# Layer A's triangular inverse: forward substitution on 16x16 blocks with a merge to 32x32, in place of forward substitution on 32x32 blocks

## The chip, the core and the metric

The kernel runs on one core of one Trainium2 chip. A core has five engines, each with its own instruction queue: TensorE (PE; its weight loads are shown apart as PEld), VectorE (DVE), ScalarE (ACT), GpSimd (POOL) and SyncE (SP), which here issues every DMA. Each takes its instructions in the order in which the program put them and waits for another engine only through semaphores. The metric is the device time of one launch in microseconds. Three runs of the kernel before gave 2158.89, 2161.75 and 2168.25 us; the median, 2161.75 us, is what a change is held against.

## What is computed

Two layers over 1024 tokens of width 1024: layer A mixes tokens with a gated delta rule, layer B with a forgetting attention. Of layer A this matters here:

```
L = where(strict, einsum('bhncd,bhnsd->bhncs', kb, k) * decay, 0.0)
T = triangular_solve(eye + L, eye, left_side=True, lower=True, unit_diagonal=True)
u = T @ vb
w = T @ (kb * exp(g)[..., None])
...
v_new = u_n - einsum('bhcd,bhde->bhce', w_n, state)
o = einsum(q_n, state) + einsum(a_n, v_new)
state = state * gl_n + einsum(k_n, v_new)
```

So every chunk of every head needs the inverse of a unit lower triangular matrix before its state update can run, and the updates of one head run one after the other. The kernel uses chunks of 128 tokens (the reference's 64 is a choice of blocking with the same result) and so inverts 128x128 matrices.

## The kernel before

Layer A is cut into 16 units: two halves of the sequence (h, 512 tokens, four chunks each) times eight pairs of value heads (g). A unit holds eight 128x128 triangular matrices (two heads times four chunks), numbered u.

For each unit the kernel (1) projects k, q and two heads of v and convolves them (`proj_conv`, and `proj_tile` for the gate z): six tiles of 24 matmuls of 128x512, which accumulate in PSUM tile `mm`; (2) builds the matrices in `lm` (`prepk`, L835); (3) inverts their diagonal blocks (`invert_blocks`); (4) merges the blocks into the whole inverse `r` (`invert_merge`, tile `rmat`); (5) runs the chain over four chunks (`chain`: PSUM tiles `ch` and `co`, with `xp`, `vn`, `ve` and `state` between them); (6) normalises and stores (`finish`). Layer A's output projection follows, then layer B.

`invert_blocks` moves the 32 diagonal 32x32 blocks of a unit (eight matrices, four blocks each) through DRAM, so that one block lies in one partition (L996 writes `lb`, L999 loads `lr`). Four groups of 32 partitions hold copies, and each copy solves every fourth column of the inverse. Forward substitution is 31 steps of two DVE instructions: a product `xtmp` (L1009) and a subtraction from `xi` (L1013). Step j has up to j // 4 + 1 columns and 31 - j rows, so 8 to 76 elements per partition. The result goes through DRAM again (L1018 writes `rb`, L1025 loads it into the diagonal blocks of `rmat`).

`invert_merge` transposes three of the four blocks on DVE (L1035, into `tmat`), merges pairs of 32 into 64 in two batches of small matmuls with ACT copies behind each (`pp`, L1043 and L1044; `rmat`, L1057 and L1059; a DVE scaling at L1058), and 64 into 128 in two more (`pq`, L1070; `rmat`, L1078). All these matmuls go to PSUM tile `su`, which has two banks; transposes on PE go to tile `tr`, also two banks.

PE's order is written by a planner inside the kernel (`Flow`). It runs the stages above as generators with priorities, adds up an estimated PE cost in `flow.t`, and fills PE with projection matmuls, which have the lowest priority, while a stage waits. A `yield` of some nanoseconds is how long the planner thinks the other engines take before the stage may go on; `flow.bank` and `flow.free` say when a PSUM bank may be used again. A merge isn't planned earlier than `LAT` ns after its inversion was issued (`t["end"]`), and later stages wait for counters (`done["merge"] >= i - 1` for `prepk`). The other engines' order comes from the tile framework's scheduler. Nearly all matmuls carry the line of the helper that records them, L121 (L125 for transposes), so they are told apart by tile.

Of the kernel before, what the change touches and what calls it, by code (L numbers as in the profile page):

```python
# [8 lines left out]
F32 = mybir.dt.float32  # L9
F32R = mybir.dt.float32r  # L10
BF16 = mybir.dt.bfloat16
AF = mybir.ActivationFunctionType
ALU = mybir.AluOpType
AX = mybir.AxisListType

P = 128
D = 1024
# [21 lines left out]
Y_PV = 6500  # L39
Y_PM = 1850  # L40
Y_P2 = 13300
Y_M0 = 900
Y_M1 = 1050
Y_M2 = 1100
# [18 lines left out]
Y_TC = 1500  # L63
ZL = 3
HI = 3000
LAT = 50000
Y_PB = 2500
Y_WO = 250
Y_WH = 3450
# [18 lines left out]
R_M = 800  # L88
# [5 lines left out]
XP = 0  # L94


class Flow:
# [36 lines left out]
    def bank(self, key, bufs, alloc):  # L134
        ring = self.rings.setdefault(key, [0, [0.0] * bufs])
        while ring[1][ring[0] % bufs] > self.t:
            yield 150
        i = ring[0] % bufs
        ring[0] += 1
        ring[1][i] = 1e15  # L140
        ps = alloc()
        self.held.append((ps, ring[1], i))
        return ps

    def free(self, ps, delay):
        n = next(n for n, v in enumerate(self.held) if v[0] is ps)
# [25 lines left out]
def tile_trunk(  # L172
# [287 lines left out]
    with ExitStack() as sa:  # L460
# [3 lines left out]
        def at(shape, name, bufs=1, dt=F32):  # L464
            return pa.tile(shape, dt, name=name, tag=name, bufs=bufs)
# [7 lines left out]
        nw_h = at([P, 1], "nw_h")  # L473
        dt_b = at([P, 16], "dt_b")
        neg_a = at([P, 16], "neg_a")
        xid = at([P, 8, 32], "xid", 1, BF16)
        nc.gpsimd.memset(xid, 0.0)
        for q in range(4):
            nc.gpsimd.affine_select(
                out=xid[32 * q : 32 * q + 32], in_=xid[32 * q : 32 * q + 32],  # L480
                compare_op=ALU.not_equal, fill=1.0, base=-q,
                pattern=[[-4, 8], [1, 32]], channel_multiplier=0,
            )
        rmat = [at([P, 8, P], f"rmat{i}") for i in range(2)]
        tmat = [at([P, 8, 64], f"tmat{i}") for i in range(2)]
        for i in range(2):
            nc.gpsimd.memset(rmat[i], 0.0)
            nc.gpsimd.memset(tmat[i], 0.0)
        halo = at([P, 32, 3], "halo")
        state = [at([P, 2 * P], f"state{g}") for g in range(NG)]  # L490
        ht_h = xt_([P, KT, HALF], "ht_h", dt=F32R)
# [2 lines left out]
        def start_norm():  # L494
# [16 lines left out]
            banks = []  # L511
            for _ in range(2):
                banks.append((yield from acc_bank()))
            for n, b in ((0, "lr"), (1, "vt")):
                br = at([1, D], b, 1)
                nc.sync.dma_start(br, ada_b[0:1, n * D : n * D + D])
                acc = at([P, D], "d2", 2)
                for k in range(KT):
# [198 lines left out]
        def proj_all():  # L717
            for i in range(2 * NG):
                h, g = divmod(i, NG)
                if g == 0:  # L720
                    if h == 0:
                        yield from start_norm()
                        done["start"] = 1
                    else:
                        yield from hold(lambda: done["norm"] == 1)
                        load_norm()
                    gt = {}
                    flow.add(gates(h, gt), 1)
# [259 lines left out]
        def invert_blocks(t):  # L988
            lm = t["lm"]
            t["r"] = r = rmat[t["g"] % 2]  # L990
            U = 2 * CPH
            lb = dram.tile([U, 4, 32, 32], F32, name="lb", tag="lb", bufs=2)
            t0 = flow.t
            for b in range(4):
                sl = slice(32 * b, 32 * b + 32)
                nc.sync.dma_start(lb[:, b].rearrange("u i j -> i u j"), lm[sl, :, sl])  # L996
            lr = at([P, 32, 32], "lr", 1)
            for q in range(4):
                nc.sync.dma_start(  # L999
                    lr[32 * q : 32 * q + 32], lb.rearrange("u b i j -> (u b) i j")  # L1000
                )
            xi = at([P, 8, 32], "xi", 1)
            nc.gpsimd.tensor_copy(xi, xid)
            for j in range(31):
                m = j // 4 + 1
                n = 31 - j
                tmp = at([P, 256], "xtmp", 1)
                tv = tmp[:, 0 : m * n].rearrange("p (m n) -> p m n", n=n)
                (nc.gpsimd if XP else nc.vector).tensor_tensor(  # L1009
                    tv, bc(lr[:, j + 1 :, j], 1, m), xi[:, 0:m, j : j + 1].broadcast_to([P, m, n]),  # L1010
                    op=ALU.mult,
                )
                (nc.gpsimd if XP else nc.vector).tensor_tensor(  # L1013
                    xi[:, 0:m, j + 1 :], xi[:, 0:m, j + 1 :], tv, op=ALU.subtract
                )
            rb = dram.tile([U, 4, 8, 4, 32], F32, name="rb", tag="rb", bufs=2)
            for q in range(4):
                nc.sync.dma_start(  # L1018
                    rb[:, :, :, q, :].rearrange("u b m i -> (u b) m i"), xi[32 * q : 32 * q + 32]
                )  # L1020
            rbv = rb.rearrange("u b m q i -> u b (m q) i")
            yield from hold(lambda: done["core"] >= done["inv"] - 1)
            for b in range(4):
                sl = slice(32 * b, 32 * b + 32)
                nc.sync.dma_start(r[sl, :, sl], rbv[:, b].rearrange("u c i -> c u i"))  # L1025
            done["inv"] += 1
            t["end"] = max(flow.t + Y_R2, t0 + LAT)

        def invert_merge(t):
            lm, r, tm = t["lm"], t["r"], tmat[t["g"] % 2]  # L1030
            U = 2 * CPH
            for b in (0, 1, 2):
                sl = slice(32 * b, 32 * b + 32)
                c0 = 32 * (b % 2)
                nc.vector.transpose(tm[sl, :, c0 : c0 + 32], r[sl, :, sl])  # L1035
            pa_ = yield from pst("su", 2)
            pb_ = yield from pst("su", 2)
            pp = at([P, U, 32], "pp", 1)
# [689 lines left out]
```

## Time and profile before

| | us |
|---|---|
| runs of the kernel, median of three | 2161.75 (2158.89 to 2168.25) |
| the profiled execution, its own time | 2165.32 |
| span of its instructions, first to last | 2163.6 |
| mean granted TensorE clock | 0.938 of full speed |
| layer A's units (first merge at 202.7, last at 1165.2) | about 100 to 1180 |
| layer A's output projection and the start of layer B | about 1180 to 1440 |
| layer B and the last projection | 1440 to 2163.6 |

The profile is one execution; its own time is 3.57 us over the median of the runs, and 1.7 us of it lie outside the span. A page of the profile gives busy time by engine, the span in 40 slices, the chain of work that ended last (followed back from the last instruction to whatever released each step), and groups of instructions with their busy time, the mean duration of one, and the idle time of the engine ahead of them. Further views give the same for a window of time, the instructions in order of time, and the waits added up. Where the names of two tiles stand as `out<-in`, the first is written and the others are read.

### The profile page before, as it was taken

The numbers are of one execution on the slowest core, as the hardware profiler recorded it, in microseconds if no ns is written. First come the engines' busy times: TensorE is split into PE (matmuls) and PEld (weight loads), VectorE is DVE, ScalarE is ACT, GpSimd is POOL, SyncE is SP. The second block draws the span as 40 slices with busy tenths as digits, with TensorE's granted clock in tenths as the row PEclk, the third lists the DMA queues.
The fourth block names the chain that finished last, engine by engine and source line by source line (L and its number), as shares of the span: only waits on it lengthen the run. The fifth ranks groups of instructions, "written<-read, shape, count | busy, mean of one in ns | idle before, by whom it ended". The sixth has DMA issues, their size and how long they took to land.

```text
span 2163.6 us, 32167 instructions
## 1 busy us (share of the span) xinstructions
PE 1865.2 (86%) x10860; PEld 1543.0 (71%) x10860; DVE 1586.1 (73%) x3625; ACT 1047.5 (48%) x2530; POOL 800.8 (37%) x648
## 2 busy tenths in 40 slices
PE   4667788888878888888888878899999999999898
PEld 3545666666667666767777756688888898888676
DVE  7788888787876888788987676745665666566664
ACT  4244444445536354445554444425655556555631
POOL 4244334344444433344442465642312322322212
PEclk7878889999999989899999999999999999999999
DMA  6544333344333323233326667611101201111522
GB/s 247 164 139 122 88 107 103 86 120 121 105 98 114 108 69 86 73 99 89 103 76 205 223 203 262 204 55 61 64 25 53 66 25 54 59 35 48 173 76 93
DMA packets 168088, 232.86 MB, mean 108 GB/s; under 512 B 66858, under 2 KB 107074, under 8 KB 167924
## 3 DMA queue, kind: packets, MB, share of 16 engines
q1 hardware_dynamic: 167924, 230.82, 34.5%
q8 instruction: 85, 1.39, 0.3%
q14 instruction: 79, 0.65, 0.1%
HBM read 203.88 MB, written 26.88 MB: 107 GB/s over the span
## 4 chain that ended last, share of the span: by engine, by line
PE 43%; DVE 30%; DMA 10%; issue 6%; ACT 5%; POOL 3%; SPq 2%; DVEq 0%; POOLq 0%; ACTq 0%
PE mm L121 26%; DVE xtmp L1009 5%; DVE xi L1013 5%; PE lg L121 5%; DVE cv_y L707 4%; PE pt L125 3%; PE oT L121 3%; PE tr L125 2%; POOL wlo L314 2%; DVE ohi L260 2%; DMA oraw<-in_ada_w_dram 2%; DMA wraw<-in_wb_dram 1%; DMA lr<-lb 1%; DMA oraw<-og_d 1%; ACT whi L311 1%
## 5 line engine op out<-in xcount | busy, mean ns | idle before, releaser
L121 PE MATMUL mm<-ht_h,whi 128*128 128x512 f32 x784 | 361.1, 461 | 5.8 <-DVE olo L287 4.4
L314 POOL TENSOR_TENSOR wlo<-wlo,whi 128x1024 fp32r<-128x1024 f32 x99 | 242.2, 2447 | 333.2 <-issue 170.4
L121 PE MATMUL mm<-ht_l,whi 128*128 128x512 f32 x784 | 323.5, 413 | 6.1 <-DVE ht_l L554 3.5
L121 PE MATMUL mm<-ht_h,wlo 128*128 128x512 f32 x784 | 322.8, 412 | 1.6 <-POOL wlo L314 1.6
L707 DVE SCALAR_TENSOR_TENSOR cv_y<-cv_t,conv_h,cv_y 128x512 f32<-128x512 f32 x192 | 194.7, 1016 | 38.3 <-ACT cv_y L699 37.2
L1009 DVE TENSOR_TENSOR xtmp<-lr,xi 128x60 f32<-128x60 f32 (+24 forms) x496 | 171.2, 345 | 28.7 <-DMA lr<-lb 13.0
L121 PE MATMUL mm<-whi,h_h 128*128 128x384 f32 x512 | 186.4, 364 | 1.6 <-ACT whi L311 1.6
L121 PEld LDWEIGHTS mm<-ht_h,wlo 128*128 128x128 f32 x784 | 157.0, 200 | 38.4 <-POOL wlo L314 2.1
L121 PEld LDWEIGHTS mm<-ht_h,whi 128*128 128x128 f32 x784 | 157.4, 201 | 37.7 <-DVE olo L287 5.2
L121 PEld LDWEIGHTS mm<-ht_l,whi 128*128 128x128 f32 x784 | 158.0, 202 | 35.5 <-DVE ht_l L554 6.5
L1312 POOL TENSOR_TENSOR rs<-ss,mhalf 128x4 f32<-128x4 f32 x64 | 64.5, 1009 | 313.3 <-DVE ss L1310 307.8
L121 PE MATMUL mm<-wlo,h_h 128*128 128x384 f32 x512 | 173.5, 339 | 3.5 <-POOL wlo L314 3.5
L121 PE MATMUL mm<-whi,h_l 128*128 128x384 f32 x512 | 172.9, 338 | 0.0
L311 ACT CAST whi<-wlo 128x1024 fp32r<-128x1024 f32 x100 | 104.7, 1047 | 134.0 <-PE mm L121 65.6
L1469 DVE TENSOR_TENSOR ptl<-pt,pth 128x512 fp32r<-128x512 f32 x192 | 106.4, 555 | 84.1 <-ACT pth L1468 82.1
L1013 DVE TENSOR_TENSOR xi<-xi,xtmp 128x60 f32<-128x60 f32 (+24 forms) x496 | 156.9, 316 | 11.1
L1468 ACT CAST pth<-pt 128x512 fp32r<-128x512 f32 x192 | 91.4, 477 | 131.1 <-PE pt L125 130.0
L1433 ACT ACTIVATE lg<-lg,mx 128x896 f32<-128x896 f32 (+7 forms) x128 | 99.5, 777 | 53.6 <-DVE mx L1425 49.4
L711 ACT ACTIVATE cv_t<-cv_y 128x512 f32<-128x512 f32 x64 | 40.4, 631 | 149.5 <-DVE cv_y L707 133.5
L314 POOL TENSOR_TENSOR wlo<-ht_h,whi 128x1024 fp32r<-128x1024 f32 x31 | 79.3, 2560 | 84.9 <-ACT whi L311 73.3
L314 DVE TENSOR_TENSOR olo<-oraw,ohi 128x256 fp32r<-128x256 f32 x96 | 80.6, 857 | 35.4 <-ACT ohi L311 32.7
L121 PEld LDWEIGHTS mm<-wlo,h_h 128*128 128x128 f32 x512 | 97.3, 190 | 7.2 <-POOL wlo L314 5.3
(340 smaller groups left out, 4924.5 us busy)
## 6 DMA issues: line engine op xcount, KB each, us to landing
wlo<-in_wa_c_dram SPq DMA_DIRECT2D x64, 512.0 KB
ht_h<-in_wa_o_dram SPq DMA_DIRECT2D x62, 512.0 KB
oraw<-in_ada_w_dram SPq DMA_DIRECT2D x128, 128.0 KB
wlo<-in_wa_z_dram SPq DMA_DIRECT2D x32, 512.0 KB
gb<-g_d SPq DMA_DIRECT2D x32, 512.0 KB
wraw<-in_wb_dram SPq DMA_DIRECT2D x56, 256.0 KB
oraw<-og_d SPq DMA_DIRECT2D x96, 128.0 KB
cumb<-cum_d SPq DMA_DIRECT2D x18, 512.0 KB
```

The source lines that it names most:

```text
L121: self.nc.tensor.matmul(out, lhsT, rhs, start=start, stop=stop)
L125: self.nc.tensor.transpose(out, src, ident)
L260: nc.vector.scalar_tensor_tensor(acc, ws[k], cond[:, k : k + 1], acc, op0=ALU.mult, op1=ALU.add)
L311: nc.scalar.copy(hi, src)
L314: (lo_eng or nc.gpsimd).tensor_tensor(lo, src, hi.bitcast(F32), op=ALU.subtract)
L707: nc.vector.scalar_tensor_tensor(y, raw[:, j : j + HALF], w[:, j : j + 1], y, op0=ALU.mult, op1=ALU.add)
L1009: (nc.gpsimd if XP else nc.vector).tensor_tensor(tv, bc(lr[:, j + 1 :, j], 1, m), xi[:, 0:m, j : j + 1].broadcast_to([P, m, n]), op=ALU.mult,)
L1013: (nc.gpsimd if XP else nc.vector).tensor_tensor(xi[:, 0:m, j + 1 :], xi[:, 0:m, j + 1 :], tv, op=ALU.subtract)
L1312: nc.gpsimd.tensor_tensor(rs, ss, mhalf[:, 0:4], op=ALU.pow)
L1433: nc.scalar.activation(lg, lg, AF.Exp, scale=-1.0, bias=mx[:, hh : hh + 1], accum_out=sums[:, tt : tt + 1],)
L1468: nc.scalar.copy(ph_[:, cs], pp[:, cs])
L1469: nc.vector.tensor_tensor(pl_[:, cs], pp[:, cs], ph_[:, cs].bitcast(F32), op=ALU.subtract)
```

## The change

The diagonal blocks that forward substitution inverts are now 16x16. A partition holds one 16x16 block: partitions come in four groups of 32 as before, groups 0 and 2 take the upper left and groups 1 and 3 the lower right 16x16 half of each 32x32 block, and each group solves every second column. That makes 15 steps of two instructions on 8 to 36 elements, in a tile `lr16` of 16x16 with two buffers; `xi` has two buffers as well, and the two instructions no longer have a switch to GpSimd.

The result goes to `rb`, now two fixed DRAM tensors `rbz` that are filled with zeros once at the start (the zeros of the off-diagonal 16x16 parts stay). The loads into `rmat` are the same four.

`invert_merge` gains a stage. It transposes four blocks instead of three, waits in the plan until all four banks of `su` and `tr` are free (`flow.both`) and takes them, runs 32 small matmuls (eight matrices, four blocks), copies the result with four ACT instructions to `qq`, runs 32 more, writes the negated result with four ACT instructions into `rmat`, and transposes three of the four blocks once more. Then it goes on as before. `Y_MQ` and `Y_MR` are the two new planned delays, 1500 and 2000 ns. `LAT` goes from 50000 to 36000. The first two bias rows of the start use another buffer, since `lr` is gone.

```diff
-LAT = 50000
+LAT = 36000
...
+    def both(self, keys):
+        while any(v > self.t for k in keys for v in self.rings[k][1]):
+            yield 100
...
+        rbz = [dram.tile([8, 4, 32, 32], F32, name=f"rb{i}", tag=f"rb{i}") for i in range(2)]
...
-            lr = at([P, 32, 32], "lr", 1)
+            lr = at([P, 16, 16], "lr16", 2)
             for q in range(4):
+                e = slice(16 * (q % 2), 16 * (q % 2) + 16)
                 nc.sync.dma_start(
-                    lr[32 * q : 32 * q + 32], lb.rearrange("u b i j -> (u b) i j")
-                )
-            xi = at([P, 8, 32], "xi", 1)
+                    lr[32 * q : 32 * q + 32], lb.rearrange("u b i j -> (u b) i j")[:, e, e]
+                )
+            xi = at([P, 8, 16], "xi", 2)
             nc.gpsimd.tensor_copy(xi, xid)
-            for j in range(31):
-                m = j // 4 + 1
-                n = 31 - j
+            for j in range(15):
+                m = j // 2 + 1
+                n = 15 - j
...
-                (nc.gpsimd if XP else nc.vector).tensor_tensor(
+                nc.vector.tensor_tensor(
                     tv, bc(lr[:, j + 1 :, j], 1, m), xi[:, 0:m, j : j + 1].broadcast_to([P, m, n]),
                     op=ALU.mult,
                 )
...
+            rbv = rbz[t["g"] % 2]
             for q in range(4):
+                e = slice(16 * (q % 2), 16 * (q % 2) + 16)
                 nc.sync.dma_start(
-                    rb[:, :, :, q, :].rearrange("u b m i -> (u b) m i"), xi[32 * q : 32 * q + 32]
-                )
+                    rbv.rearrange("u b (e m r) i -> r e (u b) m i", r=2, m=8)[q // 2, q % 2, :, :, e],
+                    xi[32 * q : 32 * q + 32],
+                )
...
         def invert_merge(t):
...
-            for b in (0, 1, 2):
-                sl = slice(32 * b, 32 * b + 32)
-                c0 = 32 * (b % 2)
-                nc.vector.transpose(tm[sl, :, c0 : c0 + 32], r[sl, :, sl])
+            for b in range(4):
+                nc.vector.transpose(tms[b], r[sls[b], :, sls[b]])
+            yield from flow.both(("su", "tr"))
+            pbk = []
+            for tag in ("su", "su", "tr", "tr"):
+                pbk.append((yield from pst(tag, 2)))
+            qq = at([P, U, 16], "qq", 1)
+            for u in range(U):
+                us = slice(u * 16, u * 16 + 16)
+                for b in range(4):
+                    o = 32 * b
+                    mm(
+                        pbk[b][o : o + 16, us], lm[sls[b], u, o : o + 16], r[sls[b], u, o + 16 : o + 32],
+                        start=True, stop=True,
+                    )
+            for b in range(4):
+                h16 = slice(32 * b, 32 * b + 16)
+                nc.scalar.copy(qq[h16], pbk[b][h16, 0 : U * 16].rearrange("p (u t) -> p u t", t=16))
+            yield Y_MQ
+            for u in range(U):
+                us = slice(U * 16 + u * 16, U * 16 + u * 16 + 16)
+                for b in range(4):
+                    h16 = slice(32 * b, 32 * b + 16)
+                    mm(pbk[b][h16, us], tms[b][0:16, u, 0:16], qq[h16, u], start=True, stop=True)
+            for b in range(4):
+                h16 = slice(32 * b, 32 * b + 16)
+                nc.scalar.mul(
+                    r[h16, :, 32 * b + 16 : 32 * b + 32],
+                    pbk[b][h16, U * 16 : U * 32].rearrange("p (u t) -> p u t", t=16), -1.0,
+                )
+                if b < 3:
+                    nc.vector.transpose(tms[b], r[sls[b], :, sls[b]])
+                flow.free(pbk[b], R_M)
+            yield Y_MR
```

How the built programs differ at the places that matter:

On DVE, before the change, the rows below are the end of one unit's substitution (`xtmp`, `xi`) and the transposes that follow it; `xp`, `ve` and `state` are the chain of an earlier unit, `zg` a gate.

```order
L1009 TENSOR_TENSOR xtmp<-lr,xi 128x16
L1013 TENSOR_TENSOR xi<-xi,xtmp 128x8x2
L1009 TENSOR_TENSOR xtmp<-lr,xi 128x8
L909 SCALAR_TENSOR_TENSOR xp<-ch,weg,vtok 128x128 x2
L1013 TENSOR_TENSOR xi<-xi,xtmp 128x8
L752 SCALAR_TENSOR_TENSOR zg<-cv_t,zg 128x512
L923 TENSOR_TENSOR ve<-ch,g_ex 128x256
L942 SCALAR_TENSOR_TENSOR state_142<-state_142,g_ex,co 128x128
L1035 STREAM_TRANSPOSE tmat_130<-rmat_128 32x8x32
L942 SCALAR_TENSOR_TENSOR state_142<-state_142,g_ex,co 128x128
L1035 STREAM_TRANSPOSE tmat_130<-rmat_128 32x8x32 x2
```

After it, at the end of a unit's substitution (lines of the changed kernel: L1022 and L1026 are the two instructions of a step, L1049 the four transposes):

```order
L1022 TENSOR_TENSOR xtmp<-lr_4205,xi 128x8
L1026 TENSOR_TENSOR xi<-xi,xtmp 128x8
L264 TENSOR_SCALAR ohi<-oraw,cond 128x256
L284 COPY gcol_89<-mm 128x2
L266 SCALAR_TENSOR_TENSOR ohi<-oraw,cond,ohi 128x256
L935 TENSOR_TENSOR ve<-ch,g_ex 128x256
L266 SCALAR_TENSOR_TENSOR ohi<-oraw,cond,ohi 128x256 x2
L952 COPY state_142<-co 128x128 x2
L266 SCALAR_TENSOR_TENSOR ohi<-oraw,cond,ohi 128x256
L1049 STREAM_TRANSPOSE tmat_130<-rmat_128 32x8x32
L899 TENSOR_TENSOR d_4317<-su,d_4317 128x512 x2
L1049 STREAM_TRANSPOSE tmat_130<-rmat_128 32x8x32 x2
```

In both, a handful of other work stands between the last step of the substitution and the transposes that need its result back from DRAM; DVE has 3157 rows before and 2622 now.

On PE, before the change, a merge begins with the batch of 32x32 matmuls that the first rows below show, between projection matmuls (`mm`):

```order
L121 MATMUL mm<-ht_h,wlo 128x512
L121 MATMUL mm<-ones,ohi 128x1 x2
L121 MATMUL su<-rmat_128,d_3845 32x32 x16
L121 MATMUL mm<-ht_h,whi 128x512
L121 MATMUL mm<-ht_l,whi 128x512
```

Now it begins with two batches of 16x16 matmuls, of which the end of the first and the start of the second are shown (`qq` is what ACT copied out in between):

```order
L123 MATMUL su<-rmat_127,d_3178 16x16 x2
L123 MATMUL tr<-rmat_127,d_3178 16x16 x2
L123 MATMUL mm<-ht_h,whi 128x512
L123 MATMUL mm<-ht_l,whi 128x512
L123 MATMUL mm<-ht_h,wlo 128x512
...
L123 MATMUL su<-qq,tmat_129 16x16 x2
L123 MATMUL tr<-qq,tmat_129 16x16 x2
```

Nine projection matmuls stand between the two batches here, and six more before the next stage that takes a bank of `su`.

More of the change, by code (lines that the diff above doesn't have):

```diff
@@ L41 @@
 Y_P2 = 13300
+Y_MQ = 1500
+Y_MR = 2000
 Y_M0 = 900
@@ L480, in tile_trunk @@
                 out=xid[32 * q : 32 * q + 32], in_=xid[32 * q : 32 * q + 32],
-                compare_op=ALU.not_equal, fill=1.0, base=-q,
-                pattern=[[-4, 8], [1, 32]], channel_multiplier=0,
+                compare_op=ALU.not_equal, fill=1.0, base=-(q // 2),
+                pattern=[[-2, 8], [1, 16]], channel_multiplier=0,
             )
@@ L513, in start_norm @@
                 banks.append((yield from acc_bank()))
-            for n, b in ((0, "lr"), (1, "vt")):
-                br = at([1, D], b, 1)
+            for n, b in ((0, ("vtok", 3)), (1, ("vt", 1))):
+                br = at([1, D], *b)
                 nc.sync.dma_start(br, ada_b[0:1, n * D : n * D + D])
@@ L723, in proj_all @@
                         done["start"] = 1
+                        for v in range(2):
+                            nc.sync.dma_start(
+                                rbz[v].rearrange("u b i j -> (u b i) j").rearrange("(p a) j -> p (a j)", p=P),
+                                rmat[v][:, 0:2].rearrange("p u t -> p (u t)"),
+                            )
                     else:
@@ L1012, in invert_blocks @@
                 )
[L1013 removed]
+                nc.vector.tensor_tensor(
                     xi[:, 0:m, j + 1 :], xi[:, 0:m, j + 1 :], tv, op=ALU.subtract
                 )
[L1016 removed]
+            rbv = rbz[t["g"] % 2]
             for q in range(4):
+                e = slice(16 * (q % 2), 16 * (q % 2) + 16)
                 nc.sync.dma_start(
[L1019 removed]
+                    rbv.rearrange("u b (e m r) i -> r e (u b) m i", r=2, m=8)[q // 2, q % 2, :, :, e],
+                    xi[32 * q : 32 * q + 32],
                 )
[L1021 removed]
             yield from hold(lambda: done["core"] >= done["inv"] - 1)
@@ L1031, in invert_merge @@
             U = 2 * CPH
-            for b in (0, 1, 2):
-                sl = slice(32 * b, 32 * b + 32)
-                c0 = 32 * (b % 2)
-                nc.vector.transpose(tm[sl, :, c0 : c0 + 32], r[sl, :, sl])
+            sls = [slice(32 * b, 32 * b + 32) for b in range(4)]
+            tms = [tm[sls[b], :, 32 * (b % 2) : 32 * (b % 2) + 32] for b in range(4)]
+            for b in range(4):
[32 more added lines that the diff above has]
+            yield Y_MR
             pa_ = yield from pst("su", 2)
```

4 lines of the change are left out of this document (2 added, 2 removed).

## Prediction

> **What bounds the kernel now.** I read the busy times by window first, since a share over the whole span mixes stages. The columns are window, length, then busy us and instruction count of PE, PEld, DVE, ACT and POOL, the granted clock, the DMA share and GB/s.
>
> ```profile
> 100.00:1180.00 1080.00, 900.07 (x5740) 722.98 (x5739) 886.93 (x2131) 514.35 (x1395) 436.07 (x365) 0.92 0.36 105
> 1180.00:1440.00 260.00, 222.53 (x991) 176.47 (x990) 180.15 (x269) 120.69 (x229) 141.83 (x82) 0.95 0.62 206
> 1440.00:2163.60 723.60, 692.45 (x3945) 604.45 (x3943) 437.43 (x1088) 378.49 (x832) 185.84 (x159) 0.99 0.19 62
> ```
>
> The change touches only layer A's units, the first row: 1080 us, with PE at 83%, DVE at 82%, and 180 us without a matmul in flight. Neither is full, so next comes the chain of work that ended last, cut to that window (shares by line):
>
> ```profile
> by line: DVE xtmp L1009 10.9%; PE mm L121 10.5%; DVE xi L1013 10.2%; issue 7.8%; DVE cv_y L707 7.7%; DMA lr<-lb 2.9%; PE su L121 2.7%; DVE d L835 2.2%; DMA rb<-xi 2.1%; DVE ohi L260 2.1%; DMA rmat<-rb 2.1%; DVE og L971 2.0%; PE co L121 1.9%
> ```
>
> The DVE groups named add up to 35.1%, the PE groups to 15.1%. So DVE sets the pace here, and the substitution (`xtmp`, `xi`) is its largest part: 21.1%, or 228 us. What PE waited for in this window says the same (us in total, times, longest):
>
> ```profile
> PE co L121 <- DVE ve L923: 39.7, 30, 3.5
> PE tr L125 <- DVE og L971: 25.9, 10, 5.2
> PE ch L121 <- DVE xp L909: 17.7, 12, 3.9
> ...
> PE su L121 <- ACT pp L1043: 13.8, 5, 5.6
> PE su L121 <- ACT rmat L1059: 9.8, 6, 2.5
> ```
>
> The first three are chain and finish steps that stand in DVE's queue behind other work.
>
> **What the substitution costs.** Its two groups in the same window (count, busy us, mean ns), and what single steps take:
>
> ```profile
> L1009 DVE TENSOR_TENSOR xtmp<-lr,xi 128x60 f32<-128x60 f32 (+24 forms) x496 | 171.2, 345 | 28.7 <-DMA lr<-lb 13.0 <-POOL xi L1003 4.7
> L1013 DVE TENSOR_TENSOR xi<-xi,xtmp 128x60 f32<-128x60 f32 (+24 forms) x496 | 156.9, 316 | 11.1
> ...
> 462.64 2.29 DVE L1009 TENSOR_TENSOR xtmp<-lr,xi 128x52 f32<-128x52 f32 x1
> 464.96 0.21 DVE L1013 TENSOR_TENSOR xi<-xi,xtmp 128x52 f32<-128x52 f32 x1
> 465.21 0.23 DVE L1009 TENSOR_TENSOR xtmp<-lr,xi 128x50 f32<-128x50 f32 x1
> 465.48 0.21 DVE L1013 TENSOR_TENSOR xi<-xi,xtmp 128x50 f32<-128x50 f32 x1
> ...
> 466.23 0.27 DVE L1009 TENSOR_TENSOR xtmp<-lr,xi 128x69 f32<-128x69 f32 x1
> 466.54 0.23 DVE L1013 TENSOR_TENSOR xi<-xi,xtmp 128x69 f32<-128x69 f32 x1
> ...
> 488.82 0.20 DVE L1009 TENSOR_TENSOR xtmp<-lr,xi 128x28 f32<-128x28 f32 x1
> 489.06 0.19 DVE L1013 TENSOR_TENSOR xi<-xi,xtmp 128x28 f32<-128x28 f32 x1
> ...
> 490.14 0.17 DVE L1009 TENSOR_TENSOR xtmp<-lr,xi 128x8 f32<-128x8 f32 x1
> 490.35 0.17 DVE L1013 TENSOR_TENSOR xi<-xi,xtmp 128x8 f32<-128x8 f32 x1
> ...
> 462.49 2.37 POOL L314 TENSOR_TENSOR wlo<-wlo,whi 128x1024 fp32r<-128x1024 f32 x1 [6.10 <-DVE rmat L1078]
> ```
>
> Per unit: (171.2 + 156.9) / 16 = 20.5 us. A pair takes 0.34 us at 8 elements, 0.39 at 28, 0.44 at 50, 0.50 at 69; I take 0.44 as the mean, so 31 pairs are 13.6 us. The other 6.9 us are rows like the one at 462.64: 2.29 us in place of some 0.24, under a POOL instruction that ran from 462.49 to 464.86.
>
> **The change, part by part.**
> *Removed:* 31 pairs become 15 of 8 to 36 elements, at 0.37 us (between the 8 and 28 rows): 5.6 us a unit. What becomes of the 6.9 us is bounded by two cases. If the waits behind POOL fall with the number of instructions, 30 of 62 keep 3.3 us, and the substitution saves 20.5 - 5.6 - 3.3 = 11.6 us. If POOL's instructions stop another DVE instruction instead, none of the 6.9 goes away, and it saves 13.6 - 5.6 = 8.0 us.
> The Trainium skill, page "SBUF — State Buffer", section "Who interferes with whom", says that a VectorE instruction with two SBUF inputs and a GpSimd instruction exclude each other for a whole instruction, in order of issue. The rows at 462.49 and 462.64 agree; by that rule POOL's work, which doesn't change, goes on stopping DVE, the lower of the two savings holds, and the sum below would come to 2109 us instead.
>
> *Added on DVE:* four transposes a unit, from this row:
>
> ```profile
> L1035 DVE STREAM_TRANSPOSE tmat<-rmat 32x256 f32<-32x256 f32 x48 | 20.8, 433 | 21.9 <-DMA rmat<-rb 21.0
> ```
>
> 4 x 0.433 = 1.7 us. Net, DVE saves 6.3 to 9.9 us a unit, 101 to 158 us over 16; I take the middle, 130, since both cases have one side of the trace for them (half of DVE's instructions stay, and they meet POOL too). Of the substitution's 328 us, 228 lay on the chain, a share of 0.69, so 130 us off DVE are worth 0.69 x 130 = **90 us** of span, with 70 and 158 (everything on the path) as ends.
>
> *Added on PE:* two batches of 32 small matmuls a unit. The nearest rows are a batch of 16 (two records each) and what follows it:
>
> ```profile
> 202.74 1.06 PE L121 MATMUL su<-rmat,d 32*32 32x32 f32 x32
> 203.74 0.80 PE L121 MATMUL mm<-ht_h,whi 128*128 128x512 f32 x1
> ...
> 206.60 0.24 PE L121 MATMUL su<-pp,tmat 32*32 32x32 f32 x1
> ```
>
> It holds PE for 1.00 us. Twice the matmuls on half the columns: I take 1.0 us a batch, 32 us in all, with 2.0 (64 us) above and half (16 us) below, as columns halve. Then the waits: each new batch, or the stage behind it, needs ACT's result. The two such waits of before cost PE 13.8 / 16 = 0.86 us and 9.8 / 16 = 0.61 us a unit; I take 0.75 for each of 32, so 24 us, with nothing and 32 x 5.6 = 179 us (the longest every time) as ends. Queued behind a waiting batch are projection matmuls, which then only fill PE later. The sum, 56 us, falls into a PE that stands idle for 180 us here; I charge PE's part of the chain against DVE's, 15.1 / 50.2 = 30%: **17 us**.
> The Trainium skill, "TensorEngine Tiling (Array Packing)", section "Key Properties", speaks against the change: switching the tiling mode drains TensorE. The weight loads of the batch at 202.74 show a pause of 0.65 us ahead of them; by that rule the 32 batches would pay it again, an estimate of 32 x 0.65 = 21 us more on PE, 6 on the path.
>
> *ACT* gets eight instructions a unit. These wrote tiles of twice the size:
>
> ```profile
> L1043 ACT COPY pp<-su x16: 343/356/363, 203.8 to 1166.0; 32x256 f32<-32x256 f32 x16
> L1057 ACT ACTIVATE rmat<-su x16: 357/373/379, 207.4 to 1168.2; 32x256 f32<-32x256 f32 x16
> ```
>
> At 0.36 us that is 2.9 us a unit, 46 us on an engine that is busy for 514 of 1080: hidden, apart from the waits priced above. If ACT were full, all 46 would show.
>
> *DMA and SP* keep four issues in each of the four steps. `lr` becomes a quarter of the bytes, in rows of 64 bytes instead of 4 KB. From the chain (start, us):
>
> ```profile
> 188.16 3.13 DMA rb<-xi
> 244.30 2.13 DMA rb<-xi
> 453.91 5.26 DMA lr<-lb
> 519.66 6.50 DMA lr<-lb
> ```
>
> `rb`, the small one in short rows, lands in 2.1 to 3.1 us, `lr` in up to 6.5. No row shows 64 bytes. On the chain `lr<-lb` is 2.9%, 31 us: between half of it gone and half as much again, plus or minus 16; I take 0. The two loads of zeros at the start lie far ahead of the first merge (202.74, above): 0. Buffering `xi` twice frees POOL from this:
>
> ```profile
> POOL xi L1003: 41.6, 11
> ```
>
> (us that POOL waited, times, for `rb` to be written before it could clear `xi`.) POOL isn't on the path: 0, up to a few us of gain. `LAT` moves a merge 14 us earlier in the plan. In its place the next thing late would be the transposes' wait for DRAM, 21.0 us in the row above; the substitution ends earlier by about as much, so I leave it at 0.
>
> **The sum.** 90 - 17 = 73 us. From the profiled execution's 2165.32 that is 2092; the median of the runs lies 3.57 lower, at 2161.75, so **2089 us** for the median.
>
> **The rivals.**
> *PE becomes the bound.* DVE falls to some 757 of 1007 us, PE keeps 900 and gains. Then the 56 us count in full and the saving stops at 90: 34 us, 2128. For it: PE is at 83% already. Against it: its idle time is mostly waits for DVE, and layer B runs at 96%.
> *The merge holds everything up (slower).* Until its second batch is through, a merge now owns all four banks of `su` and `tr`, which the key and value transposes, `prepk`, `prep2` and `finish` need; in the rows above one stage, batch to batch, took 3.86 us (202.74 to 206.60). Two more are 7.7 us a merge, 123 us in all; if all of it delays the chain, against 90 saved, it is 33 us slower: 2195. It decides from 90 / 16 = 5.6 us a merge on the path. Against it: projection matmuls stand between the stages, and in the last rows shown PE waited 0.6 to 0.9 us a stage, not 3.9.
> *The substitution was a filler.* DVE's short pairs fill gaps, and the planner's order on PE sets the pace: no change, 2155 to 2170. Against it: 21.1% of the chain.
> *It was the loop itself.* If the whole inversion is what each unit waits for, the higher saving holds, 0.69 x 158 = 109, PE's share is hidden, and half of `lr` goes: 125 us, 2037.
>
> **How the numbers follow.** Forecast (gain 40 to 115 us) 0.60; PE as the bound 0.13; the loop 0.12; filler 0.07; slower 0.08. So faster 0.85, same 0.07, slower 0.08 (0.5%, 11 us, is about what a measurement of this kernel can tell from none). The range: 2150 leaves the slower case, filler and little else out above; 2025 takes in the loop case and half of what lies between it and 158 us with nothing charged (2004). The extremes of the PE waits lie outside.
>
> **What would show it.** In the changed profile: the two substitution groups at 480 instead of 992 instructions and 90 to 145 us instead of 328; DVE in layer A 100 to 160 us lower; their part of the chain below 12%; layer A's last merge near 1095 instead of 1165; PE's waits for `ve`, `og` and `xp`, 83 us now, below 50; the two new batches at about 1 us each, with `qq` among the waits at 15 us or so. It is wrong if `qq` or the transposes' wait costs several us a merge, if `cv_y` (L707) takes up the stalls that `xtmp` loses, or if the last merge hardly moves.

## The result: slower by 0.6%, where 3.4% faster was forecast

| | us |
|---|---|
| before, median of five runs of this comparison | 2161.75 (2158.89 to 2168.25) |
| after, median of five runs | 2173.21 (2170.20 to 2180.52) |
| ratio after / before | 1.0058, 95% interval 1.0031 to 1.0085 |
| profiled execution of after, its own time / span | 2170.20 / 2168.5 |

The forecast was 2089, and the range ended at 2150. The busy times by window of the changed kernel (window, length, then PE, PEld, DVE, ACT and POOL, clock, DMA share, GB/s):

```profile
100.00:1180.00 1080.00, 909.15 (x7618) 726.67 (x7616) 761.05 (x1663) 543.51 (x1510) 424.76 (x363) 0.92 0.33 96
1180.00:1440.00 260.00, 226.69 (x1100) 181.72 (x1101) 181.84 (x270) 121.71 (x233) 139.59 (x80) 0.95 0.61 208
1440.00:2168.50 728.50, 699.74 (x3972) 608.62 (x3970) 442.85 (x1098) 381.98 (x837) 189.31 (x161) 0.99 0.20 63
```

DVE lost 126 us of work in layer A (886.93 to 761.05), as forecast, and the kernel is not faster. Its groups of instructions in that window (count, busy us, mean ns, idle time before them):

```profile
L714 DVE SCALAR_TENSOR_TENSOR cv_y<-cv_t,conv_h,cv_y 128x512 f32<-128x512 f32 x183 | 187.5, 1025 | 53.5 <-ACT cv_y L706 51.2 <-ACT qq L1065 0.2 <-ACT g_beta L642 0.2
L1022 DVE TENSOR_TENSOR xtmp<-lr,xi 128x30 f32<-128x30 f32 (+10 forms) x240 | 91.0, 379 | 18.3 <-DMA lr<-lb 12.8
L1026 DVE TENSOR_TENSOR xi<-xi,xtmp 128x30 f32<-128x30 f32 (+10 forms) x240 | 76.2, 318 | 6.0
...
L1049 DVE STREAM_TRANSPOSE tmat<-rmat 32x256 f32<-32x256 f32 x64 | 27.8, 434 | 41.3 <-DMA rmat<-rb 40.1
...
L1079 DVE STREAM_TRANSPOSE tmat<-rmat 32x256 f32<-32x256 f32 x48 | 20.7, 432 | 2.6 <-ACT rmat L1074 1.5
```

The substitution fell from 328.1 to 167.2 us. The first transposes (L1049) rose from 20.8 to 27.8, and the second ones (L1079) add 20.7; by these rows DVE does 133 us less. What DVE waited for in the window, first before, then after (us in total, times, longest):

```profile
DVE cv_y L707 <- ACT cv_y L699: 37.2, 23, 3.9
...
DVE xp L909 <- PE ch L121: 16.9, 17, 1.9
...
DVE state L942 <- PE co L121: 11.6, 13, 1.6
```

```profile
DVE cv_y L714 <- ACT cv_y L706: 51.2, 24, 4.6
DVE tmat L1049 <- DMA rmat<-rb: 40.1, 17, 6.9
DVE state L954 <- PE co L123: 35.9, 19, 12.1
...
DVE xp L921 <- PE ch L123: 29.6, 21, 4.2
```

With the transposes' 21.0 us of before, these four waits grew from 86.7 to 156.8 us. The freed DVE time became waiting, half of the growth for PE's `ch` and `co`, the chain's own matmuls: 37 of 70 us. PE, in turn, waited like this:

```profile
PE co L123 <- DVE ve L935: 34.6, 23, 4.3
...
PE tr L127 <- DVE og L983: 28.7, 9, 5.1
...
PE ch L123 <- DVE xp L921: 9.8, 10, 2.1
...
PE su L123 <- ACT qq L1065: 7.9, 4, 4.7
```

The first three are 73.1 us (83.3 before). So no wait of PE explains the loss: the new stage shows as 7.9 us. The pace of the merges shows it better. The row of the first `pp` copy of each merge gives the times of the first and the last of the 16 (it was 203.8 to 1166.0 before, 962 us):

```profile
L1089 ACT COPY pp<-su x16: 344/361/363, 191.4 to 1185.9; 32x256 f32<-32x256 f32 x16
```

The first merge comes 12 us earlier, the last 20 us later: 994 us for 15 units. Of these 20 us the spans of the two profiled executions keep 4.9 (2163.6 and 2168.5); the rest is made up behind the last merge, and no run shows how.

**One merge, followed.** The last merge of the changed kernel on PE, in order of time (start us, us):

```profile
1173.08 0.19 PE L123 MATMUL su<-rmat,d 32*16 32x16 f32 x2
...
1173.69 0.50 PE L123 MATMUL mm<-whi,ohi 128*128 128x512 f32 x1
...
1176.64 0.39 PE L123 MATMUL mm<-whi,olo 128*128 128x512 f32 x1
...
1176.95 0.19 PE L123 MATMUL su<-qq,tmat 16*16 16x16 f32 x2
1177.57 0.50 PE L123 MATMUL mm<-whi,ohi 128*128 128x512 f32 x1
...
1180.24 0.51 PE L123 MATMUL mm<-whi,ohi 128*128 128x512 f32 x1 [1.01 <-ACT ohi L317]
...
1182.71 0.79 PE L123 MATMUL mm<-whi,olo 128*128 128x512 f32 x1 [1.74 <-DVE olo L320]
...
1184.71 1.06 PE L123 MATMUL su<-rmat,d 32*32 32x32 f32 x32
```

ACT and DVE in the same stretch:

```profile
1173.79 0.54 ACT L1065 COPY qq<-su 16x128 f32<-16x128 f32 x2 [3.19 <-PE tr L123]
1174.35 0.54 ACT L1065 COPY qq<-tr 16x128 f32<-16x128 f32 x2
...
1177.67 0.56 ACT L1074 ACTIVATE rmat<-su 16x128 f32<-16x128 f32 x2 [1.08 <-PE tr L123]
1178.25 0.56 ACT L1074 ACTIVATE rmat<-tr 16x128 f32<-16x128 f32 x2
```

```profile
1177.97 1.36 DVE L1079 STREAM_TRANSPOSE tmat<-rmat 32x256 f32<-32x256 f32 x3
```

Batch one begins at 1173.08, its copies end at 1174.89, but batch two stands behind projection matmuls and begins at 1176.95. Its results are in `rmat` and `tmat` by 1179.33, but the 32x32 batch stands behind more projection work, two pieces of which wait themselves (1.01 and 1.74 us), until 1184.71. The stage takes 11.6 us here, of which its own path (each batch with the copies and transposes that need it) is 1.8 + 2.4 = 4.2; the rest is PE's order. Over all 16 merges the stretches from batch one to batch two and from there to the 32x32 batch average 3.7 and 8.0 us, 11.7 together. PE is busy during them, so no wait records this; but the chain of the unit can't start.

### The profile page after: what moved, and what is told of

Its sections match the earlier page's. It is cut to its first block, busy times and chain, and to the rows that moved or that the text cites. A ratio compares the mean times of both kernels' runs of the same rounds, so it can differ in the third digit from the quotient of the medians.

```text
span 2168.5 us, 35957 instructions
## 1 busy us (share of the span) xinstructions
PE 1890.7 (87%) x12908; PEld 1560.1 (72%) x12908; DVE 1468.0 (68%) x3177; ACT 1083.4 (50%) x2658; POOL 790.6 (36%) x648
## 5 line engine op out<-in xcount | busy, mean ns | idle before, releaser
L1515 DVE TENSOR_TENSOR ptl<-pt,pth 128x512 fp32r<-128x512 f32 x192 | 106.3, 555 | 85.1 <-ACT pth L1514 83.3
L1022 DVE TENSOR_TENSOR xtmp<-lr,xi 128x30 f32<-128x30 f32 (+10 forms) x240 | 91.0, 379 | 18.3 <-DMA lr<-lb 12.8
L123 PEld LDWEIGHTS mm<-whi,h_h 128*128 128x128 f32 x512 | 98.1, 192 | 4.2 <-ACT whi L317 1.9
```

Source lines behind the costliest of these rows:

```text
L123: self.nc.tensor.matmul(out, lhsT, rhs, start=start, stop=stop)
L1022: nc.vector.tensor_tensor(tv, bc(lr[:, j + 1 :, j], 1, m), xi[:, 0:m, j : j + 1].broadcast_to([P, m, n]), op=ALU.mult,)
L1515: nc.vector.tensor_tensor(pl_[:, cs], pp[:, cs], ph_[:, cs].bitcast(F32), op=ALU.subtract)
```

## The experiments

The theories at the start: **M**, the shorter substitution is worth what was forecast and the new stage in the merge eats it up; **F**, DVE's substitution only filled gaps. Then, for the stage: **P**, what costs is its place in PE's order (planned delays, held banks); **W**, the round trip PE, ACT, PE itself; **C**, PE's time for the small batches. Each time is a median, and the ratio is against the kernel before on the same chip (medians 2159.7 to 2162.8).

| kernel | us | ratio, 95% interval |
|---|---|---|
| no 16x16 stage (e1) | 2095.03 | 0.969, 0.9657 to 0.9724 |
| after, LAT 50000 (e2) | 2176.32 | 1.0064, 1.0043 to 1.0084 |
| before, LAT 36000 (e3) | 2245.23 | 1.0385, 1.0360 to 1.0409 |
| before, one step of 31 (e4) | 2108.06 | 0.975, 0.9726 to 0.9775 |
| e1 and the stage's plan (e5) | 2157.83 | 0.9989, 0.9974 to 1.0003 |
| e5 and its ACT and DVE work (e6) | 2176.54 | 1.0065, 1.0046 to 1.0084 |
| e5 and its PE batches (e7) | 2174.39 | 1.0061, 1.0037 to 1.0085 |
| after, no `tr` bank (e8) | 2162.69 | 1.0012, 0.9993 to 1.0031 |
| stage in a lane of its own (e9) | 2150.86 | 0.9956, 0.9940 to 0.9971 |
| after, short delays, one bank (e10) | 2187.38 | 1.0138, 1.0109 to 1.0167 |
| e1 and two delays (e11) | 2135.18 | 0.9887, 0.9859 to 0.9915 |
| e9, LAT 30000 (e12) | 2152.73 | 0.9966, 0.9949 to 0.9982 |
| e9, PE's part alone (e13) | 2139.36 | 0.9888, 0.9866 to 0.9910 |
| e9, ACT's and DVE's part alone (e14) | 2141.03 | 0.9901, 0.9878 to 0.9924 |
| e9, one copy for four (e15) | 2177.45 | 1.0063, 1.0042 to 1.0085 |
| e1, another order (e16) | 2106.37 | 0.9726, 0.9703 to 0.9750 |
| e9, lane of lower rank (e17) | 2150.49 | 0.9948, 0.9931 to 0.9966 |
| before and two delays (e18) | 2191.25 | 1.0150, 1.0129 to 1.0170 |

e1, e4, e5, e6, e7, e11, e13, e14 and e16 leave out a part of the inverse, so they price parts of the change and can't replace it.

### Does the substitution matter, or the stage?

**e1.** From after:

```diff
-            for b in range(4):
+            for b in range(3):
                 nc.vector.transpose(tms[b], r[sls[b], :, sls[b]])
-            yield from flow.both(("su", "tr"))
...
-            yield Y_MR
```

> The changed kernel without its new merge stage: 15 steps on 16x16 blocks, three transposes, LAT 36000, but no 16x16 batches, no qq, no second transposes (the off-diagonal 16x16 parts of the inverse stay zero). Theory M (the shorter substitution was worth some 70 to 90 us and the new stage eats it): 2070 to 2110 us. Theory F (the substitution was a filler, the loop through PE, ACT and DVE sets the pace): 2145 to 2165, as the kernel before, with the changed kernel's 11 us as the stage's own price.

2095.03, within M's bounds: the substitution part alone gains 68 us (of 2162.78, before's median beside it), and the stage costs 2173.21 - 2095.03 = **78 us**. In the view of the `pp` copies its merges run from 175.4 to 1088.5, 913 us, 81 less than in after:

```profile
L1057 ACT COPY pp<-su x16: 345/357/363, 175.4 to 1088.5; 32x256 f32<-32x256 f32 x16
```

In the same window as above PE now does more, and waits less for the chain. (The window takes in the start of the output projection here; from 100 to 1100 us, before that, PE is busy for 871.6 us in this kernel and for 839.0 in after.)

```profile
100.00:1180.00 1080.00, 934.67 (x5961) 752.66 (x5959) 784.35 (x1677) 549.15 (x1471) 466.80 (x382) 0.93 0.38 112
```

```profile
PE co L123 <- DVE ve L935: 23.9, 25, 2.6
```

PE's matmuls, as the profile has them, are also a little shorter. One of the three kinds of projection matmul from 100 to 1100 us, in after and in e1:

```profile
L123 PE MATMUL mm<-ht_h,wlo 128*128 128x512 f32 x698 | 288.0, 413 | 1.8 <-POOL wlo L320 1.8
...
L123 PE MATMUL mm<-ht_h,wlo 128*128 128x512 f32 x745 | 302.5, 406 | 1.1 <-POOL wlo L320 1.1
```

The other two take 466 and 412 ns in after, 452 and 404 in e1. Over some 700 of each that is about 20 us, an estimate, of the 78; the granted clock there is 0.92 and 0.93. Whether the longer matmuls follow from the chain's delay or are a cost of their own, no run separates.

**e2 and e3.** After with `-LAT = 36000 +LAT = 50000`, and before with the reverse.

> The changed kernel with LAT back at 50000: the plan puts each merge 14 us later after its inversion. If the merge now comes too early and the engines wait for the inversion's DMAs (40.1 us on DVE in place of 21.0): faster than the changed kernel, 2140 to 2160. If the plan's place of the merge doesn't matter: 2168 to 2178. Theory F and theory M both allow either.

> The kernel before with LAT at 36000 and nothing else: how much the plan's place of the merge is worth by itself, and how far a mere new order moves the time. If a merge that is planned 14 us too early makes PE wait for the 31 steps: 2180 or more. If only the order changes: 2150 to 2175.

After doesn't mind (2176.32 against 2173.21, intervals that overlap). Before loses 82 us, and the waits of PE in its layer A say why:

```profile
PE su L121 <- DMA rmat<-rb: 97.4, 19, 15.3
```

With 31 steps a unit's diagonal blocks land up to 15.3 us after PE has come to their merge. PE's order is nearly that of e1 (in the two traces 10620 of the 10860 matmuls stand at the same place), and this kernel is 150 us slower than it.

**e4.** Before, with `for j in (30,)` in place of `range(31)`, so that only the last step is left; the inverse stays nearly the identity.

> The kernel before with 1 of the 31 substitution steps (the inverse is left almost at the identity): the limit of what a shorter substitution can give, 20 us of DVE a unit and 320 us in all taken away, nothing else changed. Theory M: at least 120 us faster, below 2040. Theory F: 2110 to 2155, since PE's 1080 us in layer A hold only 180 us without a matmul and those come from the loop.

2108.06, F's number. Its two groups are down to 8.2 us from 328.1, and that is worth only 55 us. So M and F each hold for a part: at before's order 320 us off DVE are worth 55. Its merges run from 193.7 to 1106.4:

```profile
L1043 ACT COPY pp<-su x16: 343/350/364, 193.7 to 1106.4; 32x256 f32<-32x256 f32 x16
```

That is 913 us, the same as in e1, which leaves 148 us more of substitution on DVE; e1's first merge only comes 18 us earlier. So something other than DVE's substitution seems to set the pace of the merges in these two, and the 13 us that e1 has over e4 fit its earlier first merge. Before's substitution with e1's place of the merges is e3, so the earlier place needs the shorter substitution.

### What of the stage costs 78 us?

**e5.** e1, with these lines of the stage put back and no instruction of it:

```diff
+            yield from flow.both(("su", "tr"))
+            pbk = []
+            for tag in ("su", "su", "tr", "tr"):
+                pbk.append((yield from pst(tag, 2)))
+            yield Y_MQ
+            for b in range(4):
+                flow.free(pbk[b], R_M)
+            yield Y_MR
```

> The short substitution without the new 16x16 stage (which was 2095.0 us), with the stage's plan put back: the wait for su and tr, the four banks taken and held, and the two planned delays, but none of its instructions (no 16x16 batch, no copy, three transposes; the off-diagonal 16x16 parts of the inverse stay zero). Theory P (plan and held banks cost the stage's 78 us): 2150 to 2180. Theory W (the round trip over PE and ACT, instructions in order behind it, costs it): 2085 to 2110. Theory C (PE's capacity and its small batches): 2085 to 2110.

2157.83, within P's bounds. Without one added instruction, 63 of the 78 us are back, and the merges again take 981 us:

```profile
L1065 ACT COPY pp<-su x16: 347/362/364, 190.2 to 1171.3; 32x256 f32<-32x256 f32 x16
```

**e6 and e7.** e5 and the eight ACT instructions and four more transposes, on SBUF data; e5 and the two batches, the second reading `r` in place of `qq`:

```diff
-                nc.scalar.copy(qq[h16], pbk[b][h16, 0 : U * 16].rearrange("p (u t) -> p u t", t=16))
+                nc.scalar.copy(qq[h16], lm[h16, :, 0:16])
```

```diff
-                    mm(pbk[b][h16, us], tms[b][0:16, u, 0:16], qq[h16, u], start=True, stop=True)
+                    mm(pbk[b][h16, us], tms[b][0:16, u, 0:16], r[h16, u, 32 * b : 32 * b + 16], start=True, stop=True)
```

> As the plan-only kernel, with the stage's ACT and DVE instructions put back (eight 16-partition copies, one more first transpose, three second transposes), reading SBUF and not the batches' banks; no 16x16 batch on PE, so the inverse is not the reference's. Theory W in its weak form (time of ACT and DVE, 46 us and 28 us in all, lengthens the chain): plan-only plus 30 to 60. Theory P: equal to the plan-only kernel within 15. Theory C: equal to it within 15.

> As the plan-only kernel, with the stage's two batches of 32 16x16 matmuls put back on PE and the fourth transpose; the second batch reads the inverse's diagonal block, so it waits for no copy; no ACT copy and no second transposes, so the inverse is not the reference's. Theory C (PE's time in small batches): plan-only plus 30 to 60. Theory W: plan-only plus 0 to 20. Theory P: equal to the plan-only kernel within 15.

2176.54 and 2174.39: 19 and 17 us over e5, a little over P's bound of 15. They don't add up: e7 has after's order on PE and neither its copies nor its second transposes, and takes as long as after (2173.21). On that order the copies, the second transposes and the wait for them cost nothing that a measurement shows.

**e8.** After, with two blocks in each of two `su` banks:

```diff
-            yield from flow.both(("su", "tr"))
...
-            for tag in ("su", "su", "tr", "tr"):
-                pbk.append((yield from pst(tag, 2)))
+            for _ in range(2):
+                pbk += [(yield from pst("su", 2))] * 2
...
-                flow.free(pbk[b], R_M)
+                if b % 2:
+                    flow.free(pbk[b], R_M)
```

> The changed kernel with its new stage in two su banks (two blocks in each bank) and no tr bank; everything else computed as in it. Theory P in the form that the held tr banks hold up the transposes of the chain (PE's waits tr<-og 28.7 and tr<-gb 14.0 us): 2110 to 2145. If the tr banks are no cause: 2165 to 2180.

2162.69: between the two expectations, 10 us below after. The held `tr` banks, with the wait for both tiles' banks, are a small part.

**e11.** e1, with only `yield Y_MQ` and `yield Y_MR` put back.

> The short substitution without the new stage (2095.0 us), with nothing of the stage but its two planned delays, 1.5 and 2.0 us a merge: no bank held, no wait for rings, no instruction of it (the off-diagonal 16x16 parts of the inverse stay zero). Theory P2: 250 us of planned merges, so 2125 to 2150. If the held banks are what costs and not the length: 2085 to 2110.

2135.18: two planned delays, together 3.5 us a merge and 56 us over 16, cost 40 us (0.7 of them) with nothing to do in them. (The planned merge times in the expectations are `flow.t` at the end of `invert_merge` less that at its begin, added up.) Merges: 943 us.

```profile
L1059 ACT COPY pp<-su x16: 345/352/363, 184.1 to 1127.6; 32x256 f32<-32x256 f32 x16
```

**e10.** After, with the stage in one `su` bank, `Y_MQ = 500` and `Y_MR = 500`.

> The changed kernel with its stage still in the chain's lane, but in one su bank (no tr bank, no wait for both rings) and with planned delays of 0.5 and 0.5 us in place of 1.5 and 2.0; the same computation. Theory P2: 262 us of planned merges, between the 149 of 2095 us and the 324 of 2173 us: 2125 to 2150. Theory W (the real round trip PE to ACT to PE is what costs; shorter planned delays only turn into waits of PE): 2165 to 2190.

2187.38, within W's bounds, and slower than after. Where the plan leaves no time, PE stands:

```profile
PE su L123 <- ACT qq L1063: 38.8, 13, 5.8
```

13 waits of 3.0 us on average. Its stage takes 4.6 and 6.5 us on average, 11.1 together, hardly less than the 11.7 of after. So P is not a slip of two constants: the trip is there, and it is paid for either as filler that pushes the chain back or as PE's waiting.

**e18.** Before, with the two delays ahead of `yield from invert_merge(t)`.

> The kernel before (2161.75 us) with the changed kernel's two planned delays, 1.5 and 2.0 us, ahead of each merge, and nothing else; the same computation. In the planner's own time the waits and merges of the chain grow only from 336 to 353 us, since LAT's waits take most of the delays up. If it is the chain's planned length that counts, at the 0.4 us per planned us that the kernels with the short substitution show: plus 5 to 15, 2165 to 2178. If each delay of a merge costs what it cost without the stage (40 us): 2195 to 2210.

2191.25, 31 us over the kernel before on that chip (2160.11). The planned length of the chain, which grew by only 17 us here, said 5 to 15 and falls as a rule, and the 35 us and more of the other expectation are just missed; a delay in the merge costs, in both kernels, 0.55 to 0.7 of itself.

**e16**, a control: e1 with `-Y_F0 = 6900 +Y_F0 = 6400`, a finish step's delay.

> A control for what a new order alone does: the short substitution without the 16x16 stage (2095.0 us) with the planned delay Y_F0 of the finish step 6400 instead of 6900, which moves some 3000 of PE's listed rows but leaves the planned merges at 154 us (149). If order as such moves the time by tens of us: under 2080 or over 2115. If what counts is the planned length of the merges: 2085 to 2110.

2106.37, 11 us over e1. It is within the bounds for planned length, but steps of this size are what a mere change of order makes here, and the 10 us of e8 and the 17 and 19 of e6 and e7 are to be read so.

### Can the stage leave the chain?

**e9.** The stage becomes `merge16`, in one bank in place of four, with a lane of its own (a generator that the planner runs beside the chain's); the chain waits for it:

```diff
+        def merge16_all():
+            for i in range(2 * NG):
+                yield from hold(lambda: done["inv"] > i)
+                yield max(0.0, ts[i]["end"] - flow.t)
+                yield from merge16(ts[i])
...
-                yield max(0.0, ts[i]["end"] - flow.t)
+                yield from hold(lambda: "m16" in ts[i])
+                yield max(0.0, ts[i]["m16"] - flow.t)
...
+        flow.add(merge16_all(), 1, HC)
```

> The changed kernel with its new 16x16 stage taken out of the chain's lane: a lane of its own issues it as soon as the unit's diagonal blocks have landed, in one su bank, while the chain of the unit before still runs; the same computation. Theory P2 (what costs is that the stage lengthens each merge within the chain's lane: in the planner's own time 324 us for the 16 merges of the changed kernel, 197 before, 149 without the stage): 157 us of planned merges here, so 2095 plus the 17 us that the batches on PE cost over the plan alone: 2100 to 2130, faster than both kernels. Theory C2 (wherever it is issued, the stage's PE, ACT and DVE work costs it): 2150 to 2180.

2150.86: faster than both kernels, by 0.4% against before, and just above C2's lower bound, not where P put it. The place, together with the three banks fewer (e8 alone gave 10), gives back 22 of the 78 us; 56 remain. In its trace `co` waits longer for `ve` than in e1 (23.9):

```profile
PE co L123 <- DVE ve L942: 43.9, 31, 4.2
```

**e12 and e17.** e9 with `LAT = 30000`; e9 with `flow.add(merge16_all(), 3)`, so that the lane ranks behind the chain and has no head start on the other engines.

> The kernel with the stage in a lane of its own, and LAT (the planned time from a unit's first load for the inversion to its merge) 30000 instead of 36000. If the short substitution is really done by then: 2085 to 2125, at or below the own-lane kernel. If the loads and the substitution need the 36: above the own-lane kernel by 10 to 60, with PE's waits on the merge's operands longer.

> The own-lane kernel (2150.9 us) with the stage's lane behind the chain and the finish steps in the planner's order of rank (3 in place of 1) and without the scheduler's head start of 1000 on the other engines; the same computation. If the rest of the stage's cost is that its copies and transposes stand ahead of the chain's steps on ACT and DVE (PE's wait for ve 43.9 us in the own-lane kernel, 23.9 without the stage): 2115 to 2140. If it is work that has to be done anyway: 2145 to 2165.

2152.73, which neither of its expectations allowed, and 2150.49, the lowest median of the kernels that compute everything: neither latency nor rank is what's left. Nor is the wait for `ve`, which in e17 is nearly back at e1's while the time stays:

```profile
PE co L123 <- DVE ve L942: 28.8, 23, 3.4
```

**e13 and e14.** e9 without the copies and second transposes; e9 without the batches (edits as in e7 and e6).

> The own-lane kernel (2150.9 us) with only PE's part of the stage: both batches of 16x16 matmuls and the four first transposes, the second batch reading the inverse's diagonal block; no ACT copies, no second transposes, so the off-diagonal 16x16 parts of the inverse stay zero. Same order on PE as the own-lane kernel. If PE's batches (some 34 us of slots there) are what is left of the stage's cost over the 2095.0 us without it: 2125 to 2150. If ACT's and DVE's instructions are: 2095 to 2115.

> The own-lane kernel with only ACT's and DVE's part of the stage: eight 16-partition copies and seven transposes a unit, reading SBUF, and no batch on PE, so the inverse is not the reference's. If ACT's and DVE's instructions are what is left of the cost: 2125 to 2150. If PE's batches are: 2095 to 2115.

2139.36 and 2141.03: the lane with either half of the work costs 44 or 46 us over e1, with both 56. So neither half alone is the cause. Each of these times also holds what the lane's plan costs with no instruction in it; that wasn't run. If the halves added up, this common part would be 44 + 46 - 56 = 34 us.

**e15.** e9, with a first batch of 32 rows and one copy:

```diff
-            for b in range(4):
-                h16 = slice(32 * b, 32 * b + 16)
-                nc.scalar.copy(qq[h16], pbk[b][h16, 0 : U * 16].rearrange("p (u t) -> p u t", t=16))
+            nc.scalar.copy(qq, bk[:, 0 : U * 16].rearrange("p (u t) -> p u t", t=16))
```

> The own-lane kernel with one ACT copy of 128 partitions in place of four of 16 after the first batch (whose matmuls write 32 rows instead of 16, so that every partition of the bank is written); the same result. If ACT's count of instructions matters: 2125 to 2145. If not: 2145 to 2160.

2177.45, 27 us slower with less work on ACT, which neither expectation allowed. The plan changes as well (two merges are planned at 18 us in place of 9); whether that is the reason wasn't tried.

## Why the prediction was wrong

- *Substitution on DVE, 101 to 158 us less, 130 taken.* Right: DVE fell by 126 us in the window, by 133 by its rows. A unit's substitution takes 167.2 / 16 = 10.5 us, between the two cases for the stalls (8.9 and 12.5). Which case is nearer isn't settled: instructions of over 0.7 us, counted in the traces, fell from 58 to 44 while the number of instructions halved, but the other kernels with the same substitution have between 27 (e15) and 43 (e7), and 8.9 (e9) to 10.3 us a unit. The stalls do come with POOL: all 58 and all 44 end 0.02 to 0.09 us after a POOL instruction that overlaps them. The Trainium skill's page "SBUF — State Buffer", section "Who interferes with whom" (a two-input VectorE instruction and a GpSimd one that reads SBUF exclude each other), fits where the stalls lie; but the sum that it gave, 2109 us, was as wrong as the other.
- *A share of the chain of 0.69 as the price of DVE's time.* Too high. At before's order e4 takes 320 us off DVE, worth 55 us: 0.17. e1 takes 172 us off (328.1 to 155.9, its rows summed) with the merges ahead by LAT, worth 68: 0.39. With 0.69 that would have been 119. A share of the chain of waits says what was late, not what an engine's time is worth: the merges of e4 and e1 take the same 913 us, with 148 us of substitution between them.
- *LAT at 0.* Wrong as a term of its own: it is harmful by 82 us without the shorter substitution (e3) and irrelevant behind the new stage (e2), and with the shorter substitution but without the stage it may be a part of the gain. That gain without LAT's 14 us wasn't run.
- *PE: two batches at 1.0 us, waits of 0.75 us, at 30%: 17 us.* **This is the step that failed.** The batch itself was priced high (the first one above holds PE for 0.61 us, 1173.08 to 1173.69), and the waits for `qq` were 7.9 us where 15 were named as the sign. But a stage inside the merge was charged as PE's work and PE's waits, and its price is the time by which the unit's chain starts later: 11.7 us a merge from the first batch to the 32x32 batch, of which 78 / 16 = 4.9 us arrive at the end. Of the 83 us between the gain of 73 that was forecast and the loss of 10, 61 lie in this term (17 for 78) and 22 in the worth of DVE's time (90 for 68). The sentence that projection matmuls queued behind a waiting batch "only fill PE later" is where it went wrong: those matmuls are planned ahead of the batch, and push the chain behind them. The rule of the Trainium skill's page "TensorEngine Tiling (Array Packing)", section "Key Properties", that a change of tiling mode drains TensorE, would have added 6 us; no run here separates it.
- *ACT hidden.* On after's order yes (e7 against after); in a lane of its own not shown: the lane with ACT's and DVE's part alone costs 46 us (e14), the lane's plan included.
- *The rivals.* "The merge holds everything up" was the case, at a chance of 0.08. Its price was too high (123 us for 78) and the gain against it too (90 for 68). (That 78 - 68 gives the 10 us of the result is no test, since both are taken against e1.) It named the held banks first; those, with the wait for both tiles' banks, add 2157.83 - 2135.18 = 23 us to the 40 of the planned delays. "Against it: projection matmuls stand between the stages" was the mechanism and not an argument against it.
- *The signs.* Of those against the forecast one came: the last merge moved 20 us the wrong way. The transposes' wait rose by 19 us, but that is 1.2 a merge and not several; `cv_y` waited 14 us longer for ACT, but its instructions kept their length (1018 and 1025 ns), so it did not take over the stalls. Of those for the forecast, 480 instructions and DVE's fall came; the substitution took 167.2 us where 90 to 145 were named, and PE's three waits 73.1 where below 50 was. The substitution's part of the chain can't be read: the chain that ended last in after's trace reaches back only to 1179.88, behind nearly all of layer A's units.
- *The range.* Half of what lies between 2037 and 2004 would have put its lower end at 2021, not 2025. Nothing hangs on it.

Left open: the 56 us of a stage that runs off the chain. Its parts don't add up (44 and 46 make 56), the lane's plan alone wasn't run, an unrelated shuffle moves 11 us, and the one wait followed there, `co` for `ve`, is 20 us over e1's in e9 and 5 us over it in e17, while the kernel's time is the same.

## What to carry to other kernels

A stage added inside a serial chain should be priced from its elapsed time, first instruction to next stage, filler included, and not from the busy time and the waits that it adds to an engine; the filler hides the wait and delays the chain. Here 4.9 of 11.7 us a merge arrived at the end, where the busy time and the waits had been put at 1.1. Work taken off another engine can be worth far less than its share of the chain of waits says (0.17 and 0.39 where 0.69 was taken), and a delay constant in the chain is a cost even where nothing runs in it. Try the two halves of such a change apart: here the one gained 68 us and the other lost 78.

## What the runs showed of the hardware

In the changed kernel's trace the substitution's instructions, on up to 36 elements per partition in place of up to 76, are not shorter on average: 379 and 318 ns against 345 and 316. Those of under 0.7 us fell from 0.24 to 0.21 us, while the stalled ones are 44 of 480 where they were 58 of 992. Every one of these stalled instructions, and of the 35 in e1 and the 29 in e9, overlaps a POOL instruction and ends within 0.1 us after it; of the 934 others of before, 148 overlap one and are not held for as long. Whether the number of stalls goes with POOL's instructions or with DVE's stays open: with the same 480 instructions it lies between 27 and 44, where half of 58 would be 29, and no run changed POOL's work.
